# First head's inverse and recurrence two to three thirds of a block later; the down stage's residual steps two ticks later and its stores one step later

## The chip, the cores and the metric

The kernel runs on one core of a Trainium2 chip. The metric is the device time of the program in microseconds, as the median of several executions. The engines in the text are TensorE (PE, with its weight loads as PEld), VectorE (DVE), ScalarE (ACT), GpSimd (POOL), and SyncE (SP), whose instruction stream issues nearly all the DMA transfers.

## What is computed

One layer of a hybrid decoder on 2048 tokens of width 1024, in float32:

```
hn   = rms_norm(x)                         # pre_mix_norm
proj = hn @ w_in                           # one input projection for all heads
o_a  = gated_delta_rule(conv+silu(q,k,v), decay, beta)      # 4 heads, chunks of 64 tokens
o_b  = hgrn2(forget, input, q)                              # 4 heads
h    = x + rms_norm([o_a * gate, o_b * gate] @ w_out)       # post_mix_norm
u    = rms_norm(h) @ w_mlp_up                               # 1024 -> 4096
y    = relu(u)**2 @ w_mlp_down                              # 4096 -> 1024
h    = h + rms_norm(y)                                      # post_mlp_norm
out  = h + sigmoid(h @ w_gate) * rms_norm(p @ w_ple)
```

The delta rule solves, for each chunk, with the unit lower triangular matrix `a_mat = I + strict_lower(k_beta k^T * decay)`; the state `s` then goes from chunk to chunk:

```
v_new = u_n - w_n s
o     = qg_n s + qk_n v_new
s     = cd_n s + kt_n^T v_new
```

## The kernel before

**Numbers and tiles.** The tokens are cut into four quarters (q = 0 to 3) of 512. Large products run as three passes on pairs of reduced-precision halves (`fp32r`): an operand is split into a rounded half, written by ACT (L168, or L221 in place), and the rest, written by DVE (L169, or L222 in place). A product of 1024 by 128 by 512 so takes 24 matmuls of 128x512.

**Mixer stage.** A work is one block of 24 matmuls (L1227): 32 works to a quarter, 8 to a head (k, q, v, z of the delta rule, then f, i, q, g of HGRN2). For the first quarter each weight block is loaded, split (`w<-raw`) and stored for the later quarters. A block is issued as three thirds of 8 matmuls, and after each third the kernel's clock ticks once. Everything else hangs on an agenda of ticks: `gdn_mixer` and `hgrn_mixer` are generators, and the numbers in `A_STEPS` or `A_FIRST` and `B_STEPS` say on which tick (counted from the head's first block) each of their steps is issued. So the tables decide behind which block of matmuls a step's instructions stand in the streams of PE, ACT, DVE and SP; each engine works its stream in order, and what one engine needs of another it waits for at the head of its stream.

`A_FIRST` holds for one head only, the first (q = 0, h = 0). The steps of `gdn_mixer` that matter are the end of the blocked triangular inverse and the recurrence behind it:

- `xd`, `xt` (L846 to L854): the inverse's diagonal blocks go through DRAM and come back transposed by DMA;
- `xn` (L856): a DVE transpose of `xt`;
- `psp5` (L861, `pairs`): PE multiplies by `xn`; ACT copies `part5` out (L874);
- `pst5`: PE, then ACT copies back into `xt` (L881) and DVE transposes into `xn` (L883);
- `psp6`: PE, then ACT copies `part6` (L889);
- `psd6`: PE, then ACT fills `xt_full` (L895, L897);
- for each of four chunks (L901 to L920): `psa` on PE and `r` on DVE (L906); `psb` on PE and `w` on ACT (L911); `psc`, `pso` on PE and the new state on DVE (L916);
- `finish`: the gated norm of the head in eight steps.

**MLP.** The up and the down product run in two halves of the tokens (quarters 0 and 1, then 2 and 3), each by seven products of half size in the manner of Strassen. In the down stage the seven products are walked in 16 pairs each (112 pairs `j` in a half; a pair is 12 matmuls, L1294). `down_pair` (L1740 on) loads a weight tile `da` and a hidden tile `db` by DMA on SP's queue (L1753, L1755) several pairs ahead and splits both. After each of the seven products DVE adds the sums into the y tiles (L1787), POOL adds up squares (L232). When the fifth product is done (pair 80), the y of the half's first quarter is complete and `later(normed(...), MLP_STEPS)` puts the post-MLP norm and the residual on the agenda; the second quarter's follows at the end of the half. In the MLP a tick is 8 matmuls.

`normed` first makes the norm's factor (`rstd_steps`: the first two of `MLP_STEPS`, L1325 to L1335), then `residual`: at each step it prefetches the residual input `xy` of the next of eight tiles by DMA (`late`, L1314, two buffers (the default of the pool `st`), on SP's queue), scales y (L1363), adds (L1364), and issues the store of the tile of some steps before to `h2d` (L1360, or L1371 at the end; also on SP's queue). The number of steps that a store lags behind is `lag`. For the half's second quarter the same steps fall into the next stage: the up stage of half 1 (whose weight tiles `a` are loaded on SP's queue at L1602, into the ring of 16 buffers in which the y tiles lie too), or the gate stage at the end.

The tables before, as steps of the first head: transposition `xn` 30, `psp5` 33, `pst5` 34, `psp6` 36, `psd6` 37, chunks 38 to 49, `finish` 50 to 61. The residual of `normed`: ticks 7, 9, 11 to 25 after pair 80.

Of the kernel before, what the change touches and what calls it, by code (L numbers as in the profile page):

```python
# [44 lines left out]


OUT_STEPS = ((1, 5) + tuple(range(7, 15)) + (15, 27), (1, 5) + tuple(range(7, 15)) + (15, 24))
MLP_STEPS = (1, 5) + tuple(range(7, 27, 2))


A_STEPS = ((3, 6, 7, 8, 9, 10, 12, 14) + tuple(range(16, 24)) + (24, 26, 28, 30, 32, 34, 36)
           + tuple(o for c in range(38, 50, 3) for o in (c, c + 1.5, c + 2))
           + (50, 52, 54, 56, 57, 58, 60, 61))
# [3 lines left out]


A_AHEAD = (-8, -5)
A_FIRST = (3, 7.5, 8, 9, 10, 11) + A_STEPS[6:16] + (25, 28, 30, 33, 34, 36, 37) + A_STEPS[23:]  # L60

A_LAST = (A_STEPS[:16] + (24, 25, 27, 28, 29, 30, 31) + tuple(range(32, 44))
          + (44, 47, 49, 50, 51, 52, 54, 55))
# [23 lines left out]
def trunk(ctx, tc, x, xT, pT, vecs, w_in, w_ab, gdn_a_log, gdn_dt_bias, w_out, w_up, w_down,  # L87
# [38 lines left out]
    def col(r):  # L126
        return cols[:, r : r + 1]
# [96 lines left out]
    def squares(acc, src, k, name, eng=V, scratch=None):  # L224

        if acc is None:
            acc = st.tile([P, QT], F32, tag="acc", name=f"acc_{name}", bufs=3)
            S.activation(acc, src, AF.Square)
        else:
            sq = scratch() if scratch else st.tile([P, QT], F32, tag="sq", name=f"sq_{name}_{k}", bufs=1)  # L230
            S.activation(sq, src, AF.Square)  # L231
            eng.tensor_tensor(acc, acc, sq, ALU.add)  # L232
        return acc
# [337 lines left out]
    with mixers as mctx:  # L571
# [526 lines left out]
        def at(t, gen, offsets):  # L1098
            for o in offsets:
                agenda.setdefault(t + o, []).append(gen)  # L1100
# [8 lines left out]
        for q in range(NQ):  # L1109
            works.append((f"ab{q}", "ab", w_ab, q, None, None, None, None))  # L1110
            for h in range(4):
# [7 lines left out]
                elif q == 0:  # L1119
                    a_steps = A_FIRST  # L1120
                at(t, gdn_mixer(q, h, g), a_steps)
# [163 lines left out]
    def later(gen, offsets):  # L1285
        for o in offsets:
            agenda.setdefault(clock[0] + o, []).append(gen)
# [21 lines left out]
    def ytile(name):  # L1309
        return f2.tile([P, QT], F32, tag="y", name=name, bufs=16)  # L1310

    def late(src, name):
        t = st.tile([P, QT], F32, tag="late", name=name)
        nc.sync.dma_start(t, src)  # L1314
        return t
# [36 lines left out]
    def residual(q, y_of, rsb, skip, gain, dst, name, sums=None, late=late):  # L1352

        xk = late(skip(0), f"x{name}{q}_0")
        y = y_of(0)
        total, puts, lag = None, [], 2 if name == "y" else 1
        for d in range(KD):
            yield
            if len(puts) == lag:
                nc.sync.dma_start(*puts.pop(0))  # L1360
            if d + 1 < KD:
                nxt, ynxt = late(skip(d + 1), f"x{name}{q}_{d + 1}"), y_of(d + 1)
            V.scalar_tensor_tensor(y, y, col(gain + d), rsb, ALU.mult, ALU.mult)  # L1363
            V.tensor_tensor(y, y, xk, ALU.add)  # L1364
            puts.append((dst[d], y))
            if sums is not None:
                total = squares(total, y, d, f"{sums}{q}")
            xk, y = nxt, ynxt
        while puts:
            yield  # L1370
            nc.sync.dma_start(*puts.pop(0))  # L1371
        return total

    def normed(q, ys, acc, skip, gain, dst, name, sums=None, pool=None, late=late):

        rd = []
        yield from rstd_steps(acc, 1.0 / D, EPS, f"{name}{q}", rd.append, pool)
        total = yield from residual(q, lambda d: ys[d], rd[0], skip, gain, dst, name, sums, late)
        if sums is not None:
            yield from rstd_steps(total, 1.0 / D, EPS, f"{sums}{q}", partial(h1_r.__setitem__, q), pool,  # L1380
                                  lambda: tp.tile([P, QT], F32, tag="rsn", name=f"rn{q}"))
# [3 lines left out]
    def passed(q):  # L1385

        rsb = spread_load(o_r[q], f"po{q}")

        def y_of(d):
            y = ytile(f"yp{q}_{d}")  # L1390
            nc.sync.dma_start(y, yod[q][d])
            return y

        total = yield from residual(q, y_of, rsb, lambda d: xT[blk(d), tok(q)], R_POSTMIX, h1d[q], "p", "h")
        yield from rstd_steps(total, 1.0 / D, EPS, f"h{q}", row_of(h1_r, q), po, wait=True)
# [135 lines left out]
    for j, (q, d) in enumerate(order):  # L1531
# [35 lines left out]
        y = ytile(f"yo{q}_{d}") if q < 2 else tp.tile([P, QT], F32, tag="stg", name=f"yo{q}_{d}")  # L1567
# [197 lines left out]
    def down(half, between):  # L1765
# [7 lines left out]
        def end(s, pool):  # L1773
            ys = y["11"] + y["21"] if s == 0 else y["12"] + y["22"]
            later(normed(qs[s], ys, acc[s], lambda d, q=qs[s]: h1d[q][d], R_POSTMLP, h2d[qs[s]], "y", pool=pool),
                  MLP_STEPS)

# [141 lines left out]
    def embedded(q, d, rsb):  # L1919

        t = bp[0].tile([P, 2, QT], F32, tag="blk", name=f"eg{q}_{d}")
        nc.sync.dma_start(t[:, 0], ed[q][d])
        V.scalar_tensor_tensor(t[:, 0], t[:, 0], ple_w[:, d : d + 1], rsb, ALU.mult, ALU.mult)
        return t

    rsb = {q: spread_load(ple_r[q], f"pg{q}", None, "acc", 3) for q in (0, 1)}
    es, puts = {(q, 0): embedded(q, 0, rsb[q]) for q in (0, 1)}, []
    for half in range(2):
# [4 lines left out]
        for d in range(KD):  # L1933
# [3 lines left out]
            puts = []  # L1937
# [69 lines left out]
```

## Time and profile before

| | before |
|---|---|
| time, median of 3 runs | 2688.53 us (2687.17 to 2689.62) |
| profiled execution, its own time | 2688.65 us |
| its span, first to last instruction | 2686.8 us |
| mean granted TensorE clock | 0.999 |
| PE busy | 2645.4 us, 98% of the span |
| DVE busy | 2025.2 us, 75% |
| ACT busy | 1500.7 us, 56% |
| POOL busy | 105.2 us, 4% |

The busy time of an engine counts its instructions alone, without waits and without the issuing of DMA. A row of the timeline gives the start and the duration of a group of like instructions that follow each other, in microseconds from the start of the span, then engine, line, operation and tiles (written, then read), their number, and in brackets the idle time ahead of the group and the operation whose end released it. `SPq` rows are DMA issues in SP's instruction stream; their duration is that of the issue, not of the transfer. A matmul of 128x512 stands as one record; the windows view counts records and busy time by engine within a stretch.

### The profile page before, as it was taken

The page shows a single profiled execution, that of the slowest core. Times are in us where ns is not written, and L with a number is a line of the kernel's source. Part 1 is how long each engine was busy: PE and PEld are TensorE (multiplying, and loading weights), DVE is VectorE, ACT ScalarE, POOL GpSimd, SP SyncE. Part 2 cuts the span into 40 slices and gives each one's busy share as a digit, 9 for nine tenths or more (in the row PEclk, how much of TensorE's full clock was granted, in tenths as well). Part 3 has the DMA queues.
Part 4 walks back from the last instruction along what each step waited for, and adds up shares of the span by engine and source line. Part 5 has one row for each costly group of instructions (what it writes and reads, how often), then busy time and mean ns, then how long its engine had stood idle before and what let it go on. Part 6 is the DMA issues. An engine that isn't in the chain of part 4 may idle for free. (4 is left out here: it accounts for less than half of the span.)

```text
span 2686.8 us, 38439 instructions
## 1 busy us (share of the span) xinstructions
PE 2645.4 (98%) x12729; PEld 2205.6 (82%) x12729; DVE 2025.2 (75%) x4202; ACT 1500.7 (56%) x3174; POOL 105.2 (4%) x114
## 2 busy tenths in 40 slices
PE   8999999999999999999999999999999999999999
PEld 7788888888888888888888888887888888887887
DVE  6787877777787777578889977757788874577775
ACT  6665655465556456576566555555466664465431
POOL 0000000000000000000000000000000000001000
PEclk9999999999999999999999999999999999999999
DMA  8776777667656665887566676667465655677663
GB/s 279 253 257 229 238 250 234 229 204 246 216 200 222 214 220 177 295 279 275 176 216 219 212 239 221 212 198 243 154 222 178 205 195 190 198 253 247 202 226 122
DMA packets 268311, 594.11 MB, mean 221 GB/s; under 512 B 50250, under 2 KB 54824, under 8 KB 250704
## 3 DMA queue, kind: packets, MB, share of 16 engines
q1 hardware_dynamic: 268112, 591.65, 65.3%
q8 instruction: 101, 1.65, 0.3%
q14 instruction: 98, 0.80, 0.1%
HBM read 427.83 MB, written 163.70 MB: 220 GB/s over the span
## 5 line engine op out<-in xcount | busy, mean ns | idle before, releaser
L1227 PE MATMUL mm<-xt,w 128*128 128x512 f32 x3072 | 784.8, 401 | 3.2 <-DVE w L169 2.1
L1227 PEld LDWEIGHTS mm<-xt,w 128*128 128x128 f32 x3072 | 554.5, 189 | 108.1 <-DVE w L169 3.0
L1294 PE MATMUL d<-db,da 128*128 128x512 f32 x2688 | 613.2, 390 | 4.1 <-DVE db L222 2.7
L1294 PEld LDWEIGHTS d<-db,da 128*128 128x128 f32 x2688 | 503.9, 188 | 112.7 <-DVE db L222 6.0
L1294 PE MATMUL u<-t,wu 128*128 128x512 f32 x2604 | 592.8, 389 | 1.2 <-ACT wu L168 0.8
L1294 PEld LDWEIGHTS u<-t,wu 128*128 128x128 f32 x2604 | 488.4, 188 | 103.9 <-ACT wu L168 1.3
L222 DVE TENSOR_TENSOR db<-db 128x512 fp32r<-128x512 f32 x224 | 162.4, 725 | 77.4 <-ACT db L221 76.8
L221 ACT ACTIVATE db<-db 128x512 fp32r<-128x512 f32 x224 | 140.7, 628 | 84.5 <-DMA db<-hid 82.7
L1683 DVE TENSOR_TENSOR u<-u,u 128x512 f32<-128x512 f32 x224 | 150.6, 682 | 37.5 <-PE u L1294 36.8
L1724 ACT ACTIVATE u<-u 128x512 f32<-128x512 f32 x128 | 80.8, 631 | 171.9 <-DVE u L1683 171.8
L1294 PE MATMUL mmg<-h2T,wg 128*128 128x512 f32 (+1 forms) x792 | 174.8, 383 | 0.1
L1294 PEld LDWEIGHTS mmg<-h2T,wg 128*128 128x128 f32 x792 | 145.5, 188 | 29.4 <-issue 0.5
L1294 PE MATMUL mmo<-mixT,w_out 128*128 128x512 f32 x720 | 164.5, 389 | 0.4 <-DMA w_out<-rest 0.4
L1294 PEld LDWEIGHTS mmo<-mixT,w_out 128*128 128x128 f32 x720 | 135.1, 188 | 28.8 <-DMA w_out<-rest 0.8
L169 DVE TENSOR_TENSOR da<-da 128x512 fp32r<-128x512 f32 x128 | 91.9, 718 | 82.3 <-ACT da L168 81.8
L168 ACT ACTIVATE da<-da 128x512 fp32r<-128x512 f32 x128 | 80.4, 628 | 130.6 <-DMA da<-sumd 114.4
L837 DVE TENSOR_TENSOR pr_g<-xs_g,sys_g 128x16 f32<-128x16 f32 (+14 forms) x240 | 93.9, 391 | 5.5
L232 POOL TENSOR_TENSOR acc_y<-acc_y,sq_y 128x512 f32<-128x512 f32 x28 | 38.0, 1359 | 1359.9 <-ACT sq_y L231 1359.9
L169 DVE TENSOR_TENSOR wu<-a,wu 128x512 fp32r<-128x512 f32 x124 | 84.9, 687 | 5.9 <-ACT wu L168 5.9
L168 ACT ACTIVATE wu<-a 128x512 fp32r<-128x512 f32 x124 | 73.1, 621 | 25.8 <-DMA a<-in_w_up_dram 24.7
L1725 ACT ACTIVATE u<-u 128x512 f32<-128x512 f32 x128 | 80.3, 628 | 2.9
L169 DVE TENSOR_TENSOR da<-dr,da 128x512 fp32r<-128x512 f32 x96 | 66.2, 690 | 15.2 <-ACT da L168 12.5
(392 smaller groups left out, 3813.3 us busy)
## 6 DMA issues: line engine op xcount, KB each, us to landing
w<-cache_in SPq DMA_DIRECT2D x96, 1024.0 KB
db<-hid SPq DMA_DIRECT2D x224, 256.0 KB
cache_in<-w SPq DMA_DIRECT2D x32, 1024.0 KB
hid<-u SPq DMA_DIRECT2D x128, 256.0 KB
da<-sumd SPq DMA_DIRECT2D x128, 256.0 KB
a<-in_w_up_dram SPq DMA_DIRECT2D x124, 256.0 KB
hid<-ht SPq DMA_DIRECT2D x96, 256.0 KB
dr<-in_w_down_dram SPq DMA_DIRECT2D x96, 256.0 KB
```

Source lines behind the costliest of these rows:

```text
L168: S.activation(t[:, 0], raw, AF.Copy)
L169: eng.tensor_tensor(t[:, 1], raw, t[:, 0], ALU.subtract)
L221: S.activation(t[:, 0], plain(t), AF.Copy)
L222: V.tensor_tensor(t[:, 1], plain(t), t[:, 0], ALU.subtract)
L232: eng.tensor_tensor(acc, acc, sq, ALU.add)
L837: V.tensor_tensor(pr[:, :, :, 0:i], xs[:, None, :, 0:i].broadcast_to([P, 2, GC, i]), sys[:, 0:i, i : i + 2].rearrange("p j two -> p two j" ...
L1227: PE.matmul(ps, *terms[i], start=i == 0, stop=i == nt - 1)
L1294: PE.matmul(ps, a, b, start=start, stop=stop)
L1683: V.tensor_tensor(c[new], c[old], ps, ALU.add)
L1724: S.activation(c[k], c[k], AF.Relu)
L1725: S.activation(c[k], c[k], AF.Square)
```

## The change

Three numbers or tables are changed; no instruction is added or taken away.

```diff
--- before.py
+++ after.py
@@ -45,7 +45,7 @@
 
 
 OUT_STEPS = ((1, 5) + tuple(range(7, 15)) + (15, 27), (1, 5) + tuple(range(7, 15)) + (15, 24))
-MLP_STEPS = (1, 5) + tuple(range(7, 27, 2))
+MLP_STEPS = (1, 5) + tuple(range(9, 31, 2))
 
 
 A_STEPS = ((3, 6, 7, 8, 9, 10, 12, 14) + tuple(range(16, 24)) + (24, 26, 28, 30, 32, 34, 36)
@@ -57,7 +57,8 @@
 
 
 A_AHEAD = (-8, -5)
-A_FIRST = (3, 7.5, 8, 9, 10, 11) + A_STEPS[6:16] + (25, 28, 30, 33, 34, 36, 37) + A_STEPS[23:]
+A_FIRST = (3, 7.5, 8, 9, 10, 11) + A_STEPS[6:16] + (25, 28, 31, 35, 36, 38, 39) + tuple(
+    o for c in range(40, 52, 3) for o in (c, c + 1.5, c + 2)) + (52, 54, 56, 58, 59, 60, 62, 63)
 
 A_LAST = (A_STEPS[:16] + (24, 25, 27, 28, 29, 30, 31) + tuple(range(32, 44))
           + (44, 47, 49, 50, 51, 52, 54, 55))
@@ -1353,7 +1354,7 @@
 
         xk = late(skip(0), f"x{name}{q}_0")
         y = y_of(0)
-        total, puts, lag = None, [], 2 if name == "y" else 1
+        total, puts, lag = None, [], 3 if name == "y" else 1
         for d in range(KD):
             yield
             if len(puts) == lag:
```

- `A_FIRST`: the steps of the first head are now `xn` 31, `psp5` 35, `pst5` 36, `psp6` 38, `psd6` 39, chunks 40 to 51, `finish` 52 to 63. The two steps that start the DMAs (25 and 28) stay.
- `MLP_STEPS`: ticks 1 and 5 (the norm's factor) stay; the residual's steps go from 7, 9, 11 and on to 25 (ten of them) to 9, 11, 13 and on to 29 (eleven, for the longer lag)
- `lag` for the post-MLP residual is 3 instead of 2: the store of tile d is issued at the step of tile d + 3.

PE's stream in the first head, around the first steps of the inverse's end. `mm_12` and `mm_16` are blocks of the second head's projection, `at_h` and `kk_g` are products of other steps, and the number behind a row is the count of matmuls. Before:

```order
L993 MATMUL at_h0_0_3_1293<-qk_h0_0_912,keys_h0_0_2_1244 128x2x64 x2
L1227 MATMUL mm_12_0_1_1321<-xt0_0_467,w_12_0_1_1153 128x512 x3
L1227 MATMUL mm_12_0_1_1321<-xt0_1_481,w_12_0_1_1153 128x512 x3
L1227 MATMUL mm_12_0_1_1321<-xt0_2_496,w_12_0_1_1153 128x512 x2
L861 MATMUL psp5_g0_0_1330<-xn_g0_0_1181,um5_597 128x128 x2
L1227 MATMUL mm_12_0_1_1321<-xt0_2_496,w_12_0_1_1153 128x512
L1227 MATMUL mm_12_0_1_1321<-xt0_3_506,w_12_0_1_1153 128x512 x3
L1227 MATMUL mm_12_0_1_1321<-xt0_4_521,w_12_0_1_1153 128x512 x3
L1227 MATMUL mm_12_0_1_1321<-xt0_5_531,w_12_0_1_1153 128x512
L861 MATMUL pst5_g0_0_1352<-xt_g0_0_1180,part5_599 128x128 x2
L993 MATMUL at_h0_0_4_1361<-qk_h0_0_912,keys_h0_0_3_1297 128x2x64 x2
```

With the change:

```order
L804 MATMUL kk_g0_1_2_1367<-y_qg0_1_1222,y_kg0_1_1152 128x128
L1228 MATMUL mm_12_0_1_1321<-xt0_5_531,w_12_0_1_1153 128x512 x2
L1228 MATMUL mm_12_0_1_1321<-xt0_6_539,w_12_0_1_1153 128x512 x3
L1228 MATMUL mm_12_0_1_1321<-xt0_7_545,w_12_0_1_1153 128x512 x3
L862 MATMUL psp5_g0_0_1386<-xn_g0_0_1181,um5_597 128x128 x2
L1228 MATMUL mm_16_0_1_1405<-xt0_0_467,w_16_0_1_1223 128x512 x3
L1228 MATMUL mm_16_0_1_1405<-xt0_1_481,w_16_0_1_1223 128x512 x3
L1228 MATMUL mm_16_0_1_1405<-xt0_2_496,w_16_0_1_1223 128x512 x2
L862 MATMUL pst5_g0_0_1414<-xt_g0_0_1180,part5_599 128x128 x2
L994 MATMUL at_h0_0_5_1423<-qk_h0_0_912,keys_h0_0_4_1349 128x2x64 x2
L709 MATMUL t_vg0_1_1438<-cst_89,y_vg0_1_1313 128x128 x4
L1228 MATMUL mm_16_0_1_1405<-xt0_2_496,w_16_0_1_1223 128x512
```

`psp5` stood behind the first third of block `mm_12`; it now stands behind the whole block and behind `kk_g`, which it was ahead of. `pst5` follows it after one third of `mm_16`, as it did after one third of `mm_12`.

ACT's stream at the end of the same head's inverse. `w_24` is the split of a weight block, `xs1` a square sum on the next quarter's input, `um6` and `vt` are operands of the second head. Before:

```order
L822 ACTIVATE um5_597<-u_g0_1_1373 32x2x32 x2
L889 ACTIVATE part6_600<-psp6_g0_0_1423 64x2x64 x2
L824 ACTIVATE um6_598<-u_g0_1_1373 64x2x64 x2
L1051 ACTIVATE vt_g0_1_1448<-t_vg0_1_1443,inv_g0_1_1262 128x128
L168 ACTIVATE w_24_0_1_1407<-raw_24_0_1_1317 128x1024
L1051 ACTIVATE vt_g0_1_1448<-t_vg0_1_1443,inv_g0_1_1262 128x128 x3
L609 ACTIVATE xs1_1_1_1342,ss2_x1_1169<-xs1_1_1_1342 128x512
L897 ACTIVATE xt_full_601<-psd6_g0_0_1461 64x2x64 x2
```

With the change:

```order
L1052 ACTIVATE vt_g0_1_1443<-t_vg0_1_1438,inv_g0_1_1262 128x128 x4
L896 ACTIVATE xt_full_601<-xt_g0_0_1180 64x4x64 x2
L169 ACTIVATE w_24_0_1_1398<-raw_24_0_1_1317 128x1024
L610 ACTIVATE xs1_1_1_1335,ss2_x1_1169<-xs1_1_1_1335 128x512
L890 ACTIVATE part6_600<-psp6_g0_0_1467 64x2x64 x2
L825 ACTIVATE um6_598<-u_g0_1_1357 64x2x64 x2
L939 ACTIVATE th_h0_1_1488<-mm_16_0_1_1405 128x256 x2
L610 ACTIVATE xs1_2_0_1394,ss2_x1_1169<-xs1_2_0_1394 128x512
L1073 ACTIVATE f_h0_1_1491<-th_h0_1_1488,hb_98,ha_96 128x512
L1074 ACTIVATE qk_h0_1_1492<-th_h0_1_1488,ha_96,hna_97 128x512
L898 ACTIVATE xt_full_601<-psd6_g0_0_1511 64x2x64 x2
```

The split `w_24` and one `xs1` square stood behind `part6`; they now stand ahead of it, and `vt` is whole ahead of both.

SP's stream of DMA issues in the down stage of half 0, at the residual of quarter 0. `da_0_j` and `db_0_j` are the loads of pair j, `xy0_d` those of the residual's input, `h2d0_d` the stores. Before:

```order
L1314 DMA xy0_1_18710<-h1d0_1_138 128x512
L1753 DMA da_0_88_18718<-sumd8_1_7400 128x512
L1755 DMA db_0_88_18720<-hid1_0_8_15489 128x512
L1753 DMA da_0_89_18738<-sumd9_1_7872 128x512
L1755 DMA db_0_89_18740<-hid1_0_9_15685 128x512
L1314 DMA xy0_2_18746<-h1d0_2_139 128x512
L1753 DMA da_0_90_18762<-sumd10_1_8301 128x512
L1755 DMA db_0_90_18764<-hid1_0_10_15893 128x512
L1360 DMA h2d0_0_169<-y11_0_0_17474 128x512
L1314 DMA xy0_3_18775<-h1d0_3_140 128x512
```

With the change:

```order
L1315 DMA xy0_1_18742<-h1d0_1_138 128x512
L1754 DMA da_0_90_18758<-sumd10_1_8301 128x512
L1756 DMA db_0_90_18760<-hid1_0_10_15893 128x512
L1315 DMA xy0_2_18770<-h1d0_2_139 128x512
L1754 DMA da_0_91_18782<-sumd11_1_9332 128x512
L1756 DMA db_0_91_18784<-hid1_0_11_16071 128x512
L1315 DMA xy0_3_18798<-h1d0_3_140 128x512
L1754 DMA da_0_92_18806<-sumd12_1_9750 128x512
L1756 DMA db_0_92_18808<-hid1_0_12_16253 128x512
L1754 DMA da_0_93_18826<-sumd13_1_10203 128x512
L1756 DMA db_0_93_18828<-hid1_0_13_16421 128x512
L1361 DMA h2d0_0_169<-y11_0_0_17474 128x512
```

`xy0_2` stood behind the loads of pair 89, and now stands behind those of pair 90; the first store `h2d0_0` stood behind pair 90, and now stands behind pair 93.

## The prediction, made before the changed kernel was run

> **What bounds the kernel now.** I read the clock of the core first, then the busy shares, then the list of what PE waited for, and last the timeline at each wait that the change touches.
>
> ```profile
> core 0: 2686.8 us, clock 0.999
> PE 2645.4 (98%) x12729; PEld 2205.6 (82%) x12729; DVE 2025.2 (75%) x4202; ACT 1500.7 (56%) x3174; POOL 105.2 (4%) x114
> 1700.00:1740.00 40.00, 40.00 (x178) 33.15 (x177) 30.48 (x49) 21.69 (x37) 0.00 (x0) 1.00 0.67 222
> PE psp_g L861 <- DVE xn_g L856: 3.0, 1, 3.0
> PE psc_g L914 <- ACT w_g L911: 3.7, 5, 1.0
> ```
>
> PE is busy for 98% of the span, so the kernel lasts as long as PE's stream. A full stretch holds 178 matmuls in 40 us, 0.2247 us each. No matmul is added or taken away; a reordering can only change the time in which PE stands or runs slowly. The work is to find how much of that lies at the places that the change moves. The list's columns are total, times, longest: the first head's single wait for `xn` is 3.0 us. Times of one execution are compared with the profiled execution's own, 2688.65 us, of which 2686.8 is span and 1.85 lies around it; it is within 0.12 of the median.
>
> **The first head, now.** Four PE rows, the DVE row of the transposition, and the windows view before and after the wait (its columns after the length: busy time and count of PE, PEld, DVE, ACT, POOL, then the granted clock).
>
> ```profile
> 111.14 2.09 PE L1227 MATMUL mm<-xt,w 128*128 128x512 f32 x8
> 116.25 1.19 PE L861 MATMUL psp_g<-xn_g,um 128*128 128x128 f32 x4 [3.01 <-DVE xn_g L856]
> 117.09 3.26 PE L1227 MATMUL mm<-xt,w 128*128 128x512 f32 x8
> 120.19 0.61 PE L861 MATMUL pst_g<-xt_g,part 128*128 128x128 f32 x4
> 115.67 0.44 DVE L856 STREAM_TRANSPOSE xn_g<-xt_g 128x256 f32<-128x256 f32 x1
> 110.00:115.00 5.00, 3.24 (x17) 2.38 (x15) 3.18 (x13) 4.95 (x16) 1.01 (x1) 1.00 0.97 324
> 115.00:120.00 5.00, 3.75 (x12) 3.21 (x13) 2.89 (x7) 2.63 (x9) 0.00 (x0) 0.66 0.95 368
> ```
>
> From 111.14 to 120.19 are 9.05 us. In them PE does 16 large matmuls (16 x 0.2247 = 3.60) and one group of four small ones (0.45 from start to start at full speed): 4.05 us. The loss is 5.0 us: 3.0 of standing, and 2.0 because the granted clock is 0.66 behind the wait, so that the same eight matmuls take 3.26 instead of 2.09.
>
> The Trainium skill ("TensorE: Matmul & The Clock Gate", "What's actually happening") says that PE falls to half its clock after a window of about 3.4 us without work and needs about as long to come back. By that rule the loss is the wait plus half of 3.4 us, an estimate of 4.7 us, where the rows give 5.0; the trace agrees, with a 3.01 us wait and the clock of 0.66.
>
> **The first head, with the change.** `psp5` goes behind the rest of block `mm_12` and behind `at_h` and `kk`: from the end of the first eight large matmuls at 113.2, eight more (1.8 us), four `at_h` and sixteen `kk` (at a quarter of 0.45 us each, 2.2 us) and the last eight of the block (1.8 us) bring PE to it at 119.0 by the old times. `xn` is there at 116.1. So the wait goes with 2.9 us to spare, and with it the clock's fall: **-5.0**.
>
> Late next is `psd6`, since `part6` now stands in ACT's stream behind the weight split `w_24` and one square `xs`.
>
> ```profile
> 116.44 0.63 ACT L609 ACTIVATE xs<-xs 128x512 f32<-128x512 f32 x1 [1.11 <-DMA xs<-in_x_dram]
> 120.90 0.91 ACT L881 ACTIVATE xt_g<-pst_g 32x64 f32<-32x64 f32 x4 [1.72 <-PE pst_g L861]
> 127.19 0.56 ACT L889 ACTIVATE part<-psp_g 64x128 f32<-64x128 f32 x2 [0.95 <-PE psp_g L861]
> 128.68 1.05 ACT L168 ACTIVATE w<-raw 128x1024 fp32r<-128x1024 f32 x1
> 129.63 0.88 ACT L1051 ACTIVATE vt_g<-t_vg,inv_g 128x128 f32<-128x128 f32 x3
> ```
>
> Added up in the order of ACT's stream from `pst5` at 121.3 on (a split 1.05, a square 0.63, the copies of `xt` 0.91, four `vt` some 1.2, keys and `xt_full` some 1.2), ACT comes to `w_24` near 126.6. Then 1.05 + 0.63 + 0.56 end `part6` at 128.9, which is when PE comes to `psd6` (8 large matmuls and two small groups behind `psp6`, at 126.3). The stream leaves no slack, and the square waits for its own DMA, by 1.11 us in the row above. I take that lateness, rounded: **+1.0**, between 0 and 3.0.
>
> In the recurrence one wait is there already:
>
> ```profile
> 150.33 1.28 ACT L938 ACT_TABLE_LOAD   x1
> 151.97 1.18 PE L1227 MATMUL mm<-xt,w 128*128 128x512 f32 x4
> 154.15 0.49 PE L914 MATMUL psc_g<-w_g,kt_g 128*128 128x128 f32 x2 [1.00 <-ACT w_g L911]
> ```
>
> From 151.97 to 154.15 PE does four matmuls (0.90) in 2.18 us: 1.28 lost behind a loaded ACT. In both orders two such loads stand between the copies `w` of the second and third chunk in ACT's stream; with the change fifteen rows instead of twelve lie between the copies, and the second load stands two rows ahead of the later one. I take 1.7 lost instead of 1.28, **+0.4**, between -1.28 (the wait goes) and +1.3 (a whole load more). In the last chunk, `r` comes to stand behind a weight split on DVE: **+0.5**, between 0 and 1.2. The first head then sums to -5.0 + 1.0 + 0.4 + 0.5 = **-3.1** us, between -6.3 and +0.5.
>
> **The down stage of half 0.** SP's issues, what releases them, and PE.
>
> ```profile
> 1813.78 0.38 SPq L1755 DMA_DIRECT2D db<-hid  x1
> 1821.49 0.68 DVE L1364 TENSOR_TENSOR y<-y,xy 128x512 f32<-128x512 f32 x1
> 1822.20 0.32 SPq L1314 DMA_DIRECT2D xy<-h1d  x1
> 1823.09 0.38 SPq L1755 DMA_DIRECT2D db<-hid  x1
> 1827.39 0.63 ACT L221 ACTIVATE db<-db 128x512 fp32r<-128x512 f32 x1 [1.06 <-DMA db<-hid]
> 1808.61 18.32 PE L1294 MATMUL d<-db,da 128*128 128x512 f32 x80
> 1828.08 0.49 PE L1294 MATMUL d<-db,da 128*128 128x512 f32 x1 [1.14 <-ACT db L221]
> 1828.80 25.22 PE L1294 MATMUL d<-db,da 128*128 128x512 f32 x108 [0.23 <-DVE db L222]
> 1855.06 7.33 PE L1294 MATMUL d<-db,da 128*128 128x512 f32 x31 [1.04 <-DVE db L222]
> ```
>
> A pair is 12 matmuls, 2.70 us. After pair 89's `db` at 1813.78 SP should issue pair 90 a pair later, near 1816.1; instead it stands at `xy0_2` until DVE ends the first add at 1822.17 and frees the buffer. Everything behind it in the queue is 6.5 us late. `db` of pair 90, issued at 1823.09, lands at 1827.4, and PE waits. From 1808.61 to 1855.06 PE does 189 matmuls (42.47) in 46.45 us: 4.0 lost, of which 20.19 - 18.20 = 2.0 up to 1828.80 and 2.0 from there on.
>
> With the change, pair 90 is ahead of `xy0_2` and is issued in time; the block falls on pair 91. The first add comes about 1.3 us later (two splits of 0.68, of pair 89, now go ahead of it), so SP is free near 1823.5. The `db` of pair 91, third issue behind, starts near 1824.4, takes the 4.3 us of pair 90's (1823.09 to 1827.39) and two splits (0.63 + 0.69): ready near 1830.0. PE comes to it at 1808.61 + 81 x 0.2247 + 2.70 = 1829.5. I take 0.5 lost there instead of 2.0 (0 to 2.0), and 1.0 instead of 2.0 in the second part, as one split less runs late into the stretch where DVE also adds the sums (0.5 to 2.5). So **-2.5**, between -3.5 and +0.5.
>
> That second part has a price of its own:
>
> ```profile
> 1846.09 0.68 DVE L222 TENSOR_TENSOR db<-db 128x512 fp32r<-128x512 f32 x1
> 1848.48 1.30 POOL L232 TENSOR_TENSOR acc_y<-acc_y,sq_y 128x512 f32<-128x512 f32 x1 [41.65 <-ACT sq_y L231]
> 1848.60 1.72 DVE L222 TENSOR_TENSOR db<-db 128x512 fp32r<-128x512 f32 x1
> ```
>
> A split of 0.68 takes 1.72 while a POOL add of 1.30 runs. The Trainium skill ("SBUF — State Buffer", on the shared port pair) says that DVE and GpSimd hold that pair in turn for a whole instruction and the loser stands still. The trace agrees (1.72 against 0.68 + 1.30 - 0.12 = 1.86). By this rule a residual add pushed later into the POOL adds would lose up to 1.3 us, which speaks against the change; the upper bound that I took for the second part does not rest on it.
>
> **The down stage of half 1** has the same order.
>
> ```profile
> 2425.77 18.89 PE L1294 MATMUL d<-db,da 128*128 128x512 f32 x81
> 2444.89 3.36 PE L1294 MATMUL d<-db,da 128*128 128x512 f32 x12 [0.23 <-DVE db L222]
> 2448.47 22.09 PE L1294 MATMUL d<-db,da 128*128 128x512 f32 x96 [0.22 <-DVE db L222]
> 2470.72 4.64 PE L1294 MATMUL d<-db,da 128*128 128x512 f32 x19 [0.17 <-DVE db L222]
> ```
>
> Losses against 0.2247 a matmul: 19.12 - 18.20 = 0.9, 3.58 - 2.70 = 0.9, 22.25 - 21.57 = 0.7. The first two are the late pairs behind the block and go nearly whole; the third I leave but for 0.1: **-1.9**, between -2.5 and 0.
>
> **The residuals of quarters 1 and 3** fall into the up stage of half 1 and the gate stage. There SP's queue also carries the up weights `a`:
>
> ```profile
> 1900.40 31.94 PE L1294 MATMUL u<-t,wu 128*128 128x512 f32 x140
> 1915.26 7.97 SPq L1602 DMA_DIRECT2D a<-in_w_up_dram  x4
> 1932.59 12.76 PE L1294 MATMUL u<-t,wu 128*128 128x512 f32 x55 [0.26 <-DVE u L1683]
> 1943.77 0.63 ACT L168 ACTIVATE wu<-a 128x512 fp32r<-128x512 f32 x1 [0.21 <-DMA a<-in_w_up_dram]
> ```
>
> 32.19 - 31.46 = 0.7 is lost behind the four loads that stood for 7.97 us. The stores of `h2d1`, whose tiles share the weights' ring, come later, and `a11_1_3` now also waits for one of them. Its split, done near 1945.1, is wanted near 1947.8 (one group of 84 matmuls behind the group before): 2.7 us of cover. If that cover is gone each further us is lost. I take **0**, between -0.7 and the third rival. The gate stage's operands of quarter 3 show no PE wait in the trace; 0.
>
> **Sum:** -3.1 - 2.5 - 1.9 = -7.5, so 2688.65 - 7.5 = **2681.2 us** (0.28% faster). About 0.2% (5.4 us) is what a measurement of this kernel can tell from no change.
>
> **The rivals.**
> *First, the first head's stall only moves.* If the square ahead of `part6` is 3 us late, `psd6` waits 3.0, the clock falls, and all 5.0 is paid there. For it: no slack by ACT's sum. Against it: only 1.11 of lateness in the nearest row. Then -2.5 - 1.9 = -4.4: 2684.2 us. Chance 0.15.
> *Second, the block only moves from pair 90 to pair 91* with its whole loss, since six transfers start at once behind it. For it: the block itself stays, as two buffers make it. Against it: pair 91 is due a pair later. The MLP then gives 0, and -3.1 is left: 2685.5 us. Chance 0.17.
> *Third, slower: the up weights wait for the later stores.* If `a11_1_3` is held as long as `a` in the row above, 7.97 us, PE loses 7.97 - 2.7 = 5.3 and, as that is over the 3.0 at which the clock fell, 2.0 more; the next group's loads stand behind the last stores in the same way. 2 x 7.3 = 14.6 against -7.5: 2695.8 us. It decides once the store is over 2.7 us late. Against it: the store ahead is issued several us before the load. Chance 0.08.
> *Fourth, all losses go:* -5.0 - 1.28 - 4.0 - 2.5 = -12.8: 2675.9 us. Chance 0.10.
>
> **How the numbers follow.** The forecast has the remaining 0.50, and its own spread, from 2678 to 2684.5, lies for nine tenths beyond 5.4 us or close to it: faster gets 0.42 of it, same 0.08. The fourth rival is faster (0.10). The first is half a us or so from the bound and gives 0.05 to faster and 0.10 to same; the second is same (0.17), but for a 0.02 of slower. The third is slower (0.08). Faster 0.57, same 0.33, slower 0.10. The range from 2676.5 to 2688.0 leaves out half of the fourth and the third with the tail of the second, some 0.2 in all.
>
> **What would show it.** In the changed profile: the row of `psp5` without a wait and the clock at 1.00 in 115 to 120 (if 0.66 appears later in the head, the first rival); a `psd6` wait near 1 us; SP's standing one pair later in the down stage and PE's first wait there under 0.5 us; no wait for `wu` longer than before in half 1. The prediction is wrong if the waits for `part6` or `r` exceed 3 us, or if pair 91 is as late as pair 90 was.

## The result

The changed kernel took 2683.01 us (median of 22 runs, 2676.21 to 2686.14) where the kernel before took 2688.14 in the runs beside it (22 runs, 2684.1 to 2692.57). The ratio is 0.998 (95% interval 0.9973 to 0.9986): 0.2% or about 5 us faster, between 3.8 and 7.3 us. The forecast was 2681.2 within 2676.5 to 2688.0. The execution that was profiled is one of the shorter ones: its own time is 2679.72 us and its span 2677.9, 8.9 us under the span before. A tick is a third of a block: in the changed first head the transposition `xn` stands one third later and everything from `psp5` on two thirds, not two to three as the title has it.

From the page of the changed kernel, its clock and its list of PE's waits (total, times, longest):

```profile
PE 2642.6 (99%) x12729; PEld 2205.4 (82%) x12729; DVE 2022.5 (76%) x4202; ACT 1501.3 (56%) x3174; POOL 105.8 (4%) x114
PE psc_g L915 <- ACT w_g L912: 6.3, 7, 2.0
```

`psp_g` is gone from the list; `psc_g` has grown from 3.7 us in five waits to 6.3 in seven.

The first head now, PE with the transposition on DVE and the window in which the clock had fallen:

```profile
110.56 3.91 PE L1228 MATMUL mm<-xt,w 128*128 128x512 f32 x16
118.39 0.61 PE L862 MATMUL psp_g<-xn_g,um 128*128 128x128 f32 x4
118.75 2.09 PE L1228 MATMUL mm<-xt,w 128*128 128x512 f32 x8
126.49 2.09 PE L1228 MATMUL mm<-xt,w 128*128 128x512 f32 x8
128.63 0.71 PE L862 MATMUL psd_g<-xt_g,part 128*128 128x128 f32 x4
114.92 0.43 DVE L857 STREAM_TRANSPOSE xn_g<-xt_g 128x256 f32<-128x256 f32 x1
115.00:120.00 5.00, 5.00 (x34) 4.44 (x33) 5.00 (x15) 2.64 (x8) 0.00 (x0) 1.00 0.96 336
```

`xn` ends at 115.35 and PE comes to `psp5` at 118.39, 3.0 us later. No wait is left, the clock in 115 to 120 is 1.00, and eight large matmuls take 2.09 us. `psd6` starts 2.14 us behind the eight matmuls at 126.49 that take 1.80: 0.3 lost, in place of the 1.0 that I had put there. The recurrence (the four chunks with `psa`, `psb`, `psc`) pays more:

```profile
151.10 1.18 PE L1228 MATMUL mm<-xt,w 128*128 128x512 f32 x4
153.20 0.49 PE L915 MATMUL psc_g<-w_g,kt_g 128*128 128x128 f32 x2 [0.92 <-ACT w_g L912]
159.40 1.17 PE L1228 MATMUL mm<-xt,w 128*128 128x512 f32 x4
162.62 0.49 PE L915 MATMUL psc_g<-w_g,kt_g 128*128 128x128 f32 x2 [2.05 <-ACT w_g L912]
161.25 1.06 ACT L169 ACTIVATE w<-raw 128x1024 fp32r<-128x1024 f32 x1 [2.41 <-DMA cache_in<-w]
162.22 0.35 ACT L912 ACTIVATE w_g<-psb_g,ncc_g 128x128 f32<-128x128 f32 x1
```

The third chunk loses 2.10 - 0.90 = 1.2 us, as before (1.28). The last chunk, which lost nothing before, loses 3.22 - 0.90 = 2.3: its copy `w` stands on ACT behind the split of a weight block (`w_12` of the third head), and that split itself stood 2.41 us for a store of an older weight, whose buffer it takes.

The down stage of half 0, SP and DVE around the blocked load, then PE:

```profile
1810.55 0.38 SPq L1756 DMA_DIRECT2D db<-hid  x1
1815.87 1.28 DVE L1365 TENSOR_TENSOR y<-y,xy 128x512 f32<-128x512 f32 x2
1816.57 0.32 SPq L1315 DMA_DIRECT2D xy<-h1d  x1
1802.63 43.17 PE L1295 MATMUL d<-db,da 128*128 128x512 f32 x189
1846.64 35.45 PE L1295 MATMUL d<-db,da 128*128 128x512 f32 x155 [0.84 <-DVE db L223]
```

SP still stands until DVE's first add, from 1810.93 to 1816.57: 5.6 us, where it stood 8.0 before (1814.16 to 1822.20). Now it is pair 91 that is behind it, and PE runs through all 189 matmuls without a wait. The same stretch that lost 4.0 us takes, with the wait of 0.84 at its end, 44.01 us for 42.47: 1.5 lost.

Half 1 with the same order did not gain in this execution:

```profile
2430.77 0.32 SPq L1315 DMA_DIRECT2D xy<-h1d  x1
2431.19 1.35 SPq L1754 DMA_DIRECT2D da<-sumd  x1
2433.60 0.37 SPq L1754 DMA_DIRECT2D da<-sumd  x1
2439.64 0.63 ACT L169 ACTIVATE da<-da 128x512 fp32r<-128x512 f32 x1 [3.47 <-DMA da<-sumd]
2416.79 23.76 PE L1295 MATMUL d<-db,da 128*128 128x512 f32 x104
2440.95 0.49 PE L1295 MATMUL d<-db,da 128*128 128x512 f32 x1 [0.39 <-ACT db L222]
2441.67 19.33 PE L1295 MATMUL d<-db,da 128*128 128x512 f32 x84 [0.23 <-DVE db L223]
2461.71 35.43 PE L1295 MATMUL d<-db,da 128*128 128x512 f32 x155 [0.71 <-DVE db L223]
```

Here the issue behind the block took 1.35 us instead of 0.37, and the `da` of pair 92, issued at 2433.60, landed 6.0 us later. Pair 91 came in time and pair 92 did not: 44.92 us for 42.47, 2.5 lost, as before the change. The up stage of half 1, with the weight loads and the residual of quarter 1 beside it, runs without a break here:

```profile
1891.99 98.26 PE L1295 MATMUL u<-t,wu 128*128 128x512 f32 x432
```

One loss of this execution lies ahead of all these places and ahead of the first step that the change moves. PE waits 1.92 us for a weight split, and the clock falls behind it:

```profile
95.73 4.61 PE L1228 MATMUL mm<-xt,w 128*128 128x512 f32 x12 [1.92 <-DVE w L170]
95.00:100.00 5.00, 4.27 (x12) 3.36 (x13) 5.00 (x9) 1.09 (x2) 0.00 (x0) 0.66 0.64 208
```

In the profile before, PE waits 1.50 us at the same matmul, and no slow clock follows.

### The profile page after: what moved, and what is told of

Same layout as the page of the kernel before. It is cut to its first block, busy times and chain, and to the rows that moved or that the text cites. A ratio compares the mean times of both kernels' runs of the same rounds, so it can differ in the third digit from the quotient of the medians.

```text
span 2677.9 us, 38473 instructions
## 1 busy us (share of the span) xinstructions
PE 2642.6 (99%) x12729; PEld 2205.4 (82%) x12729; DVE 2022.5 (76%) x4202; ACT 1501.3 (56%) x3174; POOL 105.8 (4%) x114
## 4 chain that ended last, share of the span: by engine, by line
PE 67%; DVE 15%; DMA 10%; ACT 4%; issue 2%; SPq 1%; POOL 1%; POOLq 0%; DVEq 0%; ACTq 0%
PE u L1295 22%; PE d L1295 19%; PE mm L1228 11%; PE mmg L1295 6%; PE mmo L1295 3%; DVE pr_g L838 2%; DVE xs_g L841 2%; DMA da<-sumd 2%; DMA ud_g<-u_g 2%; DMA sys_g<-ud_g 1%; PE mme L196 1%; DVE xs_g L843 1%; DMA mixT<-mixd 1%; DMA m_g<-sd_g 1%; DMA gf_g<-gd 1%
```

## The experiments

The places are compared by two measures that do not depend on where else an execution differs. The *head* is the time from the 265th to the 721st large matmul of the mixer stage, which holds the same work in every kernel. The *halves* are, for 240 matmuls of each down stage from pair 83 on, the time above 0.2247 us a matmul. Both come from the one profiled execution of each kernel, the times from all its executions. A star marks a table of the change that was edited further.

| kernel | head table | steps from | lag | head, us | half 0, us lost | half 1, us lost | time, us | ratio to before (95%) |
|---|---|---|---|---|---|---|---|---|
| before | old | 7 | 2 | 156.2 | 4.2 | 2.8 | 2688.1 | 1 |
| the change | new | 9 | 3 | 151.9 | 1.8 | 2.7 | 2683.0 | 0.998 (0.9973 to 0.9986) |
| head table only | new | 7 | 2 | 152.4 | 4.4 | 3.5 | 2683.1 | 0.9992 (0.9983 to 1.0) |
| down stage only | old | 9 | 3 | 156.2 | 1.2 | 0.5 | 2682.7 | 0.9987 (0.9979 to 0.9996) |
| steps only | old | 9 | 2 | 156.9 | 0.7 | 1.2 | 2682.1 | 0.9988 (0.9979 to 0.9997) |
| lag only | old | 7 | 3 | 156.0 | 2.3 | 2.3 | 2683.6 | 0.9991 (0.9983 to 1.0) |
| last chunk earlier | new* | 9 | 3 | 153.1 | 1.6 | 1.5 | 2681.8 | 0.9986 (0.9975 to 0.9996) |
| last chunk later | new* | 9 | 3 | 154.3 | 1.7 | 1.8 | 2679.8 | 0.9976 (0.9967 to 0.9985) |
| `psp5` at 34 | new* | 9 | 3 | 159.7 | 1.6 | 0.8 | 2686.3 | 1.0006 (0.9997 to 1.0015) |
| steps from 11 | new | 11 | 3 | 151.1 | 0.6 | 0.5 | 2677.4 | 0.9968 (0.9959 to 0.9977) |
| steps from 13 | new | 13 | 3 | 151.0 | 0.5 | 0.5 | 2677.9 | 0.9974 (0.9965 to 0.9983) |
| steps from 11, old head | old | 11 | 3 | 157.1 | 1.6 | 0.5 | 2681.5 | 0.9982 (0.9973 to 0.9991) |
| steps from 11, lag 2 | new | 11 | 2 | 153.0 | 0.5 | 0.5 | 2678.2 | 0.9968 (0.9958 to 0.9978) |
| steps from 11, last chunk later | new* | 11 | 3 | 152.0 | 0.6 | 0.5 | 2676.6 | 0.9971 (0.996 to 0.9982) |

Each ratio is against the kernel before on the same chip, whose median was 2685.8, 2686.2 and 2687.5 beside the three groups of four; so ratios, not times, are compared across groups, and a difference between two such ratios is less sure than either.

### The parts by themselves

Head table only (`A_FIRST` of the change, the rest as before):

```diff
-A_FIRST = (3, 7.5, 8, 9, 10, 11) + A_STEPS[6:16] + (25, 28, 30, 33, 34, 36, 37) + A_STEPS[23:]
+A_FIRST = (3, 7.5, 8, 9, 10, 11) + A_STEPS[6:16] + (25, 28, 31, 35, 36, 38, 39) + tuple(
+    o for c in range(40, 52, 3) for o in (c, c + 1.5, c + 2)) + (52, 54, 56, 58, 59, 60, 62, 63)
```

> Only the first head's table is changed; steps and lag of the down stage are as before. Theory: PE no longer stands at psp5 (5.0 us with the clock's fall), but the copy w of the last chunk comes behind the split of w_12 on ACT, and the first head nets -2 to -3 us between block counts 0 and 420 of the mixer's large matmuls; both down-stage halves lose 4.0 and 2.5 us as before; the time is 2 to 3 us below before. Rival: the new wait is an accident of one execution; then no psc wait over 1.3 us, the head nets -4.5 or more. Second rival: the head gains nothing (0) because the stall only moves.

The wait for `xn` is gone, and the one at the last chunk is there again:

```profile
161.84 0.49 PE L915 MATMUL psc_g<-w_g,kt_g 128*128 128x128 f32 x2 [1.74 <-ACT w_g L912]
1821.40 0.50 PE L1295 MATMUL d<-db,da 128*128 128x512 f32 x1 [0.96 <-ACT db L222]
1848.70 13.48 PE L1295 MATMUL d<-db,da 128*128 128x512 f32 x58 [1.24 <-DVE db L223]
```

So it is no accident of one execution. From the 265th up to the 421st matmul, where the expectation ends, it takes 53.5 us against 56.2: 2.7 less, as expected. Up to the 721st it takes 152.4 against 156.2, 3.8 less. The halves lose 4.4 and 3.5 us, about what they lost before, and at the same two places in half 0. The time is 0.08% below before (0 to 0.17%): the expected 2 to 3 us are inside, no change at its edge.

Down stage only (both edits of the MLP):

```diff
-MLP_STEPS = (1, 5) + tuple(range(7, 27, 2))
+MLP_STEPS = (1, 5) + tuple(range(9, 31, 2))
-        total, puts, lag = None, [], 2 if name == "y" else 1
+        total, puts, lag = None, [], 3 if name == "y" else 1
```

> Only the down stage is changed (residual steps two ticks later, stores one step later); the first head is as before, with the 3 us wait for xn. Theory: half 0 loses 1.5 us instead of 4.0 over the 189 matmuls behind the norm's two; half 1 loses 1 to 2.5, depending on how long pair 92's load takes (about 4 us: under 1.5; about 6: 2.5); the up stage of half 1 loses 0 instead of 0.7; together 3 to 4 us below before. Rival: half 0's gain is an accident of when the transfers landed, and both halves lose 2.5 to 4: not over 1 us below before.

Half 0 loses 1.2 and half 1 loses 0.5 us where the whole change, with the same order in both, lost 1.8 and 2.7. So half 1 can gain with this order; in the first profile the load of 6.0 us took the gain. How often that happens, one more execution does not tell; four others are below. The time is 0.13% below before (0.04 to 0.21%).

Steps only, with the lag of two:

```diff
+MLP_STEPS = (1, 5) + tuple(range(9, 29, 2))
```

> Only the residual's steps go two ticks later; the stores lag two steps as before. Theory: the order of xy loads against the pair loads does the work, so half 0 loses about 1.5 us as with the whole change, and the store's place (one more store between the pair loads behind the block) adds at most 0.5. Rival: the stores, of 256 KB each, ahead of pairs 92 and 93 are what makes those pairs late; then half 0 loses 2.5 or more.

Both halves lose 0.7 and 1.2 us; the later steps do the work without the later stores.

Lag only, with the steps from 7 on:

```diff
+MLP_STEPS = (1, 5) + tuple(range(7, 29, 2))
+        total, puts, lag = None, [], 3 if name == "y" else 1
```

> Only the stores lag three steps instead of two; the residual's steps stay. Theory: SP stands at xy0_2 ahead of pair 90 as before, 6 us late, and half 0 loses 2 us at pair 90 as before; the store's later place takes at most 1 us from the 4.0 of half 0. Rival: the lag is what gains; half 0 loses under 2.

```profile
1805.78 18.33 PE L1294 MATMUL d<-db,da 128*128 128x512 f32 x80
1824.84 0.51 PE L1294 MATMUL d<-db,da 128*128 128x512 f32 x1 [0.73 <-ACT db L221]
```

The wait at pair 90 stays, as expected, but half 0 loses 2.3 us and not the 3 or more that I expected: the later wait, 1.04 us at 1855.06 before, is not there. SP stands 7.2 us, from 1811.34 to 1818.50. In this execution the stores' later place alone took that second loss. By these single executions the two edits overlap: either takes the second wait, only the steps take the first.

### The first head's new waits

The last chunk's second step half a tick earlier (50 instead of 50.5), so that its copy `w` stands ahead of the split of `w_12`:

```diff
-    o for c in range(40, 52, 3) for o in (c, c + 1.5, c + 2)) + (52, 54, 56, 58, 59, 60, 62, 63)
+    o for c in (40, 43, 46) for o in (c, c + 1.5, c + 2)) + (49, 50, 51) + (52, 54, 56, 58, 59, 60, 62, 63)
```

> The changed kernel, with the last chunk of the first head's recurrence half a tick earlier at its second step and a whole tick shape of 49, 50, 51 instead of 49, 50.5, 51, so that its copy w stands ahead of the split of w_12 on ACT. Theory: that split waits for its buffer (the store of an older weight) and the copy behind it cost PE 2.0 us at the last psc; with the copy ahead the wait falls under 0.6 us, and the mixer's large matmuls 360 to 420 take about 20 us instead of 22.2 (19.0 before the change). Rival: the copy waits for PE's own psb or for r on DVE, and the wait at psc stays over 1.5 us or moves to psb.

```profile
152.56 0.49 PE L915 MATMUL psc_g<-w_g,kt_g 128*128 128x128 f32 x2 [1.77 <-ACT w_g L912]
158.45 0.49 PE L910 MATMUL psb_g<-r_g,xt_full 128*128 128x128 f32 x2 [1.05 <-DVE r_g L907]
```

The wait at the last `psc` is gone, so the split in front of the copy was its cause. But PE now waits at `psb`, for `r` on DVE: that is the wait which my prediction had named there. Matmuls 360 to 420 take 22.6 us, not the expected 20, and the head is 153.1, not shorter. The rival is right that the wait moves.

The last chunk one tick later instead:

```diff
-    o for c in range(40, 52, 3) for o in (c, c + 1.5, c + 2)) + (52, 54, 56, 58, 59, 60, 62, 63)
+    o for c in (40, 43, 46, 50) for o in (c, c + 1.5, c + 2)) + (53, 55, 57, 59, 60, 61, 62, 63)
```

> The changed kernel, with the last chunk of the first head's recurrence (and its gated norm) one tick later, the copy w still behind the split of w_12 on ACT. Theory: PE comes to the last psc 8 matmuls (1.8 us) later while the split ends at the same time, so the wait of 2.0 falls to under 0.5 us. Rival: what holds the copy moves along with the recurrence, and the wait stays over 1.5 us.

```profile
152.09 0.49 PE L915 MATMUL psc_g<-w_g,kt_g 128*128 128x128 f32 x2 [1.78 <-ACT w_g L912]
```

The last chunk's wait goes, as the theory says. The third chunk's is 1.78 in this execution and 1.77 in the one above; with the table of the change it is 0.92, 0.90, 0.76 and 0.62 in four kernels, but 1.77 in a fifth (steps from 11, lag 2). So it varies between executions of the same table. The head took 154.3 us: what the last chunk gained did not reach the head's end. Behind the wait of 1.78 the clock fell (the window below), which it did not do behind the 1.77 of the kernel above; and the second head's `psa` waits 1.70 us, 0.65 in the profile of the change.

```profile
150.00:155.00 5.00, 3.22 (x14) 2.47 (x13) 4.76 (x12) 4.33 (x9) 1.04 (x1) 0.80 0.31 79
```

With steps from 11 the same edit was tried again:

> The changed kernel with steps from 11 and the last chunk of the first head's recurrence one tick later. Theory: the wait at the last psc (1.4 to 2.0 us) goes, but PE is earlier at the third chunk's copy w behind two table loads or its wait grows by as much (it was 1.8 with the late last chunk, 0.8 to 0.9 without), so that the sum of the two waits stays near 2 us and the time is within 1.5 us of the kernel without it. Rival: the last wait goes and the third chunk's stays at 0.9; 1.5 us or more faster.

```profile
161.44 0.49 PE L915 MATMUL psc_g<-w_g,kt_g 128*128 128x128 f32 x2 [0.31 <-ACT w_g L912]
```

The last wait is 0.31 and the third chunk's 0.98, so the sum is 1.3 and not 2, as the rival has it; the head is 152.0 and the ratio 0.9971 against 0.9968 without the edit. No difference in time can be told.

`psp5` one tick earlier, to see what a short wait costs:

```diff
-(25, 28, 31, 35, 36, 38, 39)
+(25, 28, 31, 34, 36, 38, 39)
```

> The changed kernel, with psp5 one tick earlier (34 instead of 35): PE comes to it behind 16 large matmuls, about 1.2 us ahead of the transposition. Theory (the clock falls only behind a wait of about 3 us): PE waits 1.0 to 1.4 us, the granted clock stays at 1.00 in the 5 us behind it, and the loss at this place is 1.0 to 1.5 us. Rival (any wait lets the clock fall in part): the clock in the next 5 us is under 0.9 and the loss is over 2 us. If the transposition comes earlier as well, the wait is 0.

PE, then the windows behind the two waits, then ACT:

```profile
114.94 0.68 PE L862 MATMUL psp_g<-xn_g,um 128*128 128x128 f32 x4 [1.50 <-DVE xn_g L857]
149.83 0.80 PE L915 MATMUL psc_g<-w_g,kt_g 128*128 128x128 f32 x2 [5.05 <-ACT w_g L912]
115.00:120.00 5.00, 5.00 (x35) 4.58 (x35) 4.79 (x14) 3.81 (x14) 0.00 (x0) 1.00 0.99 369
145.00:150.00 5.00, 0.17 (x1) 0.17 (x2) 4.62 (x15) 4.25 (x11) 0.00 (x0) 0.89 1.00 341
150.00:155.00 5.00, 5.00 (x18) 4.52 (x19) 4.83 (x15) 2.91 (x12) 0.00 (x0) 0.50 0.26 108
141.50 1.06 ACT L169 ACTIVATE w<-raw 128x1024 fp32r<-128x1024 f32 x1 [5.88 <-DMA cache_in<-w]
147.84 1.28 ACT L939 ACT_TABLE_LOAD   x1
```

At `psp5` it came as the theory says: a wait of 1.50 us, and the clock stays at 1.00. As a rule the theory does not hold, since the clock fell behind 1.92 and 1.78 us in the rows above. And the kernel is no faster than the one before, since ACT's order came out differently: the second chunk's copy `w` stands behind a split that stood 5.88 us for a store and behind two table loads. PE waits 5.05 us, and the clock is 0.50 for the 5 us behind it. The Trainium skill ("TensorE: Matmul & The Clock Gate", "What's actually happening") tells of half the clock after some 3.4 us without work. The 5.05 us here, with 0.50 in the next window, agree with it. The 3.01 us of the kernel before, with 0.66, are shorter than that, and so are 1.92 and 1.78; there the measurement decides. So the agreement that the prediction states is one of size only, 4.7 us against 5.0.

### The block on SP

The residual's steps two ticks later again:

```diff
-MLP_STEPS = (1, 5) + tuple(range(9, 31, 2))
+MLP_STEPS = (1, 5) + tuple(range(11, 33, 2))
```

> The changed kernel, with the residual's steps two ticks later again (11, 13 and on to 31). Theory: SP comes to the blocked xy load one to two pairs later still, stands there about 3.5 us less (2 to 3 us instead of 6), and both halves lose under 1.0 us up to the sums of the sixth product; but the last adds of the residual now fall into the stretch of the sums and of POOL's adds, so that the loss there is 1 to 2 us. Net within 1.5 us of the changed kernel. Rival: no block and no loss there, both halves under 0.8 us in all, 2 us faster than the changed kernel.

SP, PE in both halves, and DVE and POOL where the sums are:

```profile
1810.40 0.38 SPq L1756 DMA_DIRECT2D db<-hid  x1
1813.83 0.32 SPq L1315 DMA_DIRECT2D xy<-h1d  x1
1799.80 62.38 PE L1295 MATMUL d<-db,da 128*128 128x512 f32 x274
2412.66 67.51 PE L1295 MATMUL d<-db,da 128*128 128x512 f32 x297
1842.29 1.78 DVE L1365 TENSOR_TENSOR y<-y,xy 128x512 f32<-128x512 f32 x1
1841.95 1.57 POOL L233 TENSOR_TENSOR acc_y<-acc_y,sq_y 128x512 f32<-128x512 f32 x1 [0.74 <-ACT sq_y L232]
```

SP stands 3.0 us instead of 5.6, and PE runs through both halves without a wait: 0.6 and 0.5 us lost. A residual add does fall on a POOL add and takes 1.78 instead of 0.68 us, but the splits have lead enough and PE does not feel it. The theory had the block right (2 to 3 us) and the loss in the stretch of the sums wrong; the rival had it the other way round, and its 0.8 us for both halves came to 1.1. The rule of the Trainium skill ("SBUF — State Buffer", "Who interferes with whom"), that the later of the two stands still for the whole instruction, agrees with this row, and the loss that it spoke for did not reach PE. At 0.9968 (0.9959 to 0.9977) this kernel is 0.32% under the kernel before. Against the change, at 0.998 (0.9973 to 0.9986) in another group of runs, the two intervals just overlap; the three later kernels with steps from 11 or 13 and the new table stand at 0.9968 to 0.9974, which speaks for a gain.

Steps from 13:

```diff
+MLP_STEPS = (1, 5) + tuple(range(13, 35, 2))
```

> The changed kernel, with the residual's steps four ticks later than in the change (13, 15 and on to 33). Theory: SP's stand at the blocked xy load shrinks from 3.0 us (steps from 11) to none, but as both halves lose only 0.5 us each already with steps from 11, nothing is left to gain; two more residual adds fall on POOL's adds and take 1.8 instead of 0.7 us, which the splits' lead covers. Time within 1.5 us of the kernel with steps from 11, each half under 0.8 us. Rival: DVE is late for the splits in the sums' stretch, and one half loses over 1.5 us.

0.5 and 0.5 us lost; SP no longer stands at that load, and there is nothing more to gain. One residual add falls on a POOL add (1.78 us), as with steps from 11, and not two more.

Steps from 11 with the head's table as before the change, and with a lag of two:

```diff
 # old head table, lag 3
+MLP_STEPS = (1, 5) + tuple(range(11, 33, 2))
 # new head table, lag 2
+MLP_STEPS = (1, 5) + tuple(range(11, 31, 2))
```

> Steps from 11 and stores three steps late, with the first head's table as before the change. Theory: the down stage's gain (3.5 in half 0, 2.2 in half 1) is whole, the first head's wait for xn with the clock's fall is back; large matmuls 264 to 720 take about 156 us instead of 152; the time is about 4 us above the kernel with both. Rival: the first head's net is under 1.5 us, as two new waits for w took the gain.

> The changed kernel with steps from 11 and the stores two steps late as before the change. Theory: the steps alone do the work, and both halves lose 0.5 to 1.0 us as with the lag of three; the time is within 1.5 us of that kernel. Rival: the stores, now nearer to the block, hold pair 91 or 92, and a half loses over 1.5 us.

```profile
114.10 0.68 PE L861 MATMUL psp_g<-xn_g,um 128*128 128x128 f32 x4 [3.22 <-DVE xn_g L856]
```

The old table brings the wait back at 3.22 us and the head to 157.1 us. Half 0 loses 1.6 us in this execution, 1.0 more than its neighbours, and these runs do not show why. The ratio of 0.9982 is 0.08 to 0.14% above the three kernels with the new table that ran beside it (0.9968 to 0.9974): 2 to 4 us, at most the expected 4, and the intervals overlap. With a lag of two the ratio is the same as with three: once the steps are late enough, the lag is worth nothing that can be measured.

## Why the prediction held, step by step

**The wait for `xn`** (-5.0): right in its mechanism and size. All five kernels with the old table wait there, for 2.85 to 3.23 us, and have a slow clock behind it; none of the five with the new one does either. It needs both terms, the 3 us of standing and the 2 us of the slow clock, as the kernel with `psp5` at 34 shows, where the standing alone is left.

**What is late next in the head** (+1.0, +0.4, +0.5): the sum of 1.9 was closer than its parts, and that was luck: 0.3, 0 and 2.3 came, 2.6 in all. `psd6` cost 0.3, not 1.0: the square ahead of `part6` was not late for its own DMA. (My sum of ACT's stream, 121.3 and the terms behind it, comes to 126.3 and not 126.6; ACT came to `w_24` at 126.32.) The third chunk cost 0, not 0.4. The last chunk cost 2.3, not 0.5, and through another engine: I had looked at `r` behind a split on DVE, and it was `w` behind a split on ACT that waited for its buffer. The DVE wait did appear once that one was taken away. The step that failed is that I read ACT's order for the third chunk and not for the last: the term was mis-sized at 0.5 where 2.3 was measured.

Over the whole head the five kernels with the old table take 156.2, 156.2, 156.9, 156.0 and 157.1 us and the five with the new one 151.9, 152.4, 151.1, 151.0 and 153.0: a mean difference of 4.6, where -3.1 was the sum (bounds -6.3 to +0.5). But this stretch is longer than the chain that the sum is about. Up to the 421st matmul, where that chain ends, the five old take 56.0 to 56.3 us and the five new 53.1 to 54.7, a mean difference of 2.5. The other 2.1 lie in the 300 matmuls behind it (100.0 to 100.8 against 97.7 to 99.0), for which the prediction had no term. There the second head's `psa`, `psb` and `pso` wait for DVE, and less so with the new table: the longest, at `psa`, is 2.59 us in the profile before and 0.65 in the one after, and from under 0.3 to 2.0 in the others with either table. Which of the moved steps brings DVE there earlier stays open. So the sum was a little too good for the chain, and what came behind it hid that.

**Half 0** (-2.5): with the steps and lag of the change, five executions lose 1.8, 1.2, 1.6, 1.7 and 1.6 against 4.2 and 4.4 without: -2.7. In the profile of the change the loss is the 1.5 us that I added up, but not at pair 91, where PE does not wait.

**Half 1** (-1.9): the same five lose 2.7, 0.5, 1.5, 1.8 and 0.8 against 2.8 and 3.5: -1.7. In the profile of the changed kernel it is next to nothing (0.1), with one load of 6.0 us. What I called the bound "to 0" is a spread between executions here.

**Quarters 1 and 3** (0): no longer wait for `wu` came of it. The 1301 matmuls of half 1's up stage lose 5.0 us before, 4.5 with the change, and 4.4 to 5.6 in the other kernels with later steps or stores, so the third rival did not occur. From the last matmul of the down stage to the end, where quarter 3's residual lies, 181.0 us pass before and 181.2 after.

**The second rival** (the block only moves): the first half of it is what happened, since SP still stands, for 5.6 us, one pair later; the loss did not move along, as pair 91 is due 2.7 us later. Steps from 11 show that the block itself could be halved, though I had taken it as fixed by the two buffers.

**The sum.** By places the means of the profiled executions give -4.6 - 2.7 - 1.7 = -9.0 us. That the two profiled spans of before and after differ by 8.9 is an accident: in these two the places give -4.3 - 2.4 - 0.1 = -6.8, and 2.1 lie outside them, where the profile before takes the longest of all fourteen (2523.6 us; the others 2519.5 to 2523.1). The measured difference over 22 runs is 5.1, between 3.8 and 7.3 us. So about 4 us of what the places show did not appear in the median. The profiled execution of the changed kernel is 3.3 us under its own median, and of the longer ones there is no profile. What is on record of them is their mean granted clock: the six of the 22 at 1.000 take 2680.4 us on average, the thirteen at 0.999 take 2683.1 and the three at 0.998 take 2685.9. A window of 5 us at 0.66, as behind the wait at 95.73, takes about 0.0006 from that mean (an estimate: 0.34 x 5 us of 2678), so three or so such falls lie between the groups at 1.000 and 0.998. Where they fall, and whether they are the whole of the rest, stays open. The forecast, -7.5, was a little too good by the runs and a little too modest by the profiles; that it lies between them owes something to errors that cancel.

## What to carry to other kernels

A step that waits at the head of an engine's stream should go behind work that is ready, but each engine's new order has to be read to the end of the moved chain: the next wait was on another engine and at the chain's other end. Where a queue in program order stands for a buffer, moving the blocked item back by one pair can hide the whole block without shortening it; look then for the position at which the block itself shrinks. A place that loses by transfers varies from execution to execution, so several profiles are needed before it is said to have gained or not.

## What the runs showed of the hardware beyond what was expected

The length of a wait of PE did not decide by itself whether the clock fell behind it. At one matmul of the mixer, ahead of every step that the edits move, all fourteen profiles have a wait for a weight split, of 1.46 to 1.92 us. Behind five of them the clock fell, behind nine it did not. Here the kernels with the down stage only and with the steps only, each with its fourteen matmuls behind the wait:

```profile
95.61 5.06 PE L1227 MATMUL mm<-xt,w 128*128 128x512 f32 x14 [1.51 <-DVE w L169]
96.64 3.46 PE L1227 MATMUL mm<-xt,w 128*128 128x512 f32 x14 [1.51 <-DVE w L169]
```

The wait is the same, and the first of the two loses 1.6 us more. Taken over all of PE's waits, the clock fell behind the six of 2.85 us and more and behind seven of the 35 between 1.2 and 2.6. What else decides, the runs do not show. To shorten a wait from 3 to 1.5 us made a fall rarer here and did not exclude it.

A shift of one small step by one tick (`psp5` at 34) cost 0.26% against the change by the two ratios, 1.0006 to 0.998; in its profile a split that waits for its buffer and a table load of 1.28 us came between a product and its copy, and the 5.05 us wait halved the clock for the next 5 us. The issue of one DMA took 1.35 us instead of 0.37 right behind a block in SP's queue, and the same load of 256 KB landed in anything from 3 to 6 us when six transfers were issued within 3 us. DVE additions with one operand in PSUM were not slowed beside POOL's adds (four in 2.48 us, 0.62 each, with steps from 11), while adds and splits with both in SBUF took 1.1 to 1.8 us instead of 0.68.
